# A hybrid decoder layer on one core: bias broadcasts moved into attention, half rows of x, and three small reorderings

## The chip, the core and the metric

The kernel runs on one core of a Trainium2 chip. A core has a matmul engine (TensorE, PE in the profile; its weight loads are PEld), three engines for elementwise work (VectorE, DVE; ScalarE, ACT; GpSimd, POOL), an engine that here only issues transfers (SyncE, SP), and 16 DMA engines that serve all transfer queues. Each engine works through its own queue in order, and semaphores make it wait for others. The metric is the device time of one execution in microseconds (us); lower is better.

## The reference

One layer (batch 1, 1024 tokens, width 1024, float32):

```python
h = rms_norm(x, attn_norm_w)
q, k, v, u, g = split(h @ w_in)                 # q, k: 8 heads x 2 halves x 64; v: 8 x 128
q, k = rms_norm(q), rms_norm(k)
p = softmax(q1 k1^T * scale + bias) - lam * softmax(q2 k2^T * scale + bias)   # causal; bias by T5 bucket of distance
a = rms_norm(p @ v, subln_w) * (1 - lam_init)
y_a = a @ w_proj_attn
c = silu(layer_norm(causal_depthwise_conv(u_a * sigmoid(u_b), conv_w, conv_b)))   # width 31
y_b = c @ w_proj_conv
x = x + (sigmoid(g_a) * y_a + sigmoid(g_b) * y_b) @ w_out
h = rms_norm(x, ffn_norm_w)
gt, up = split(h @ w_gate_up)                   # 2 x 2816 columns
x = x + (silu(gt) * up) @ w_down
```

## The kernel before

Every product is made of float32 operands split into a high and a low part (`split_hi` on ACT, L120; `split_lo` on DVE, L125, or on POOL in the first stage, L131); three matmuls (high x high, high x low, low x high) give one product. A set of weights is loaded (tile `wraw`, two buffers, or `room`), split into `whi` and `wlo`, and used. The large products, of u, of w_out and of the feed-forward part, are done with seven block products in place of eight, on sums and differences of 512 x 512 blocks; `T1` to `T4`, `S1` to `S4` are such sums. The program is unrolled. The order on each engine is set by a planner that simulates the program with its own estimates of durations; a block `with after(ins)` forces what is traced in it to stand behind `ins` on that engine's queue, and `last_of(engine)` is the instruction traced last on an engine.

The stages, with the times of the profiled execution:

- **First stage** (to about 310 us). RMSNorm and transposition of x to hT, then products of V and u, then the first of q, k. Between products, taps of the depthwise convolution (L595) fill DVE. A u item (`u_pair`) does seven products (L981); its weights are loaded by `prepare` (L945), summed by POOL (L962 to L965) and split. POOL also does the bias: it multiplies out the table of distances into b_d (8 heads x 1152), and `bias_skew(h)` (L777) broadcasts one head's row to the 128 rows of t_d[h], in DRAM, by a DMA from POOL's queue; there is one such issue per head, at every third step from n = 23 on. `add_tile` (L579) accumulates one convolution tile into cs_d, also from POOL's queue.
- **Attention** (to about 850 us). 64 steps (head h, row block i), n = 8h to 8h + 7 for head h, each with scores, exponentials, transposes of the probabilities (`turn`), and, for every two blocks, the product with V (`weigh`, tile pW). At a head's first step `load_bias(h)` reads t_d[h] with a skewed access (tile tb, L870). POOL only clears blocks of the transposed probabilities (L1318, L1319) and issues `add_tile`. Columns of g, of q and k of the later heads fill PE in between. SP loads v (vh, vl), weights, and the copies of q and k from partition to partition (qs, ks).
- **y_a and LayerNorm** (850 to about 920 us). `ya_out` (L1637) multiplies a finished product with its gate, which frees PE's bank; `ln_step` brings on steps of the LayerNorm, whose differences from the mean are L1570 and whose squares are L1571.
- **y_b, the gated merge** (to 1009 us), L1687 and L1688.
- **w_out** (1009 to 1095 us). Seven block products (L1843) in the order 11, 12, S1, S2, S4, S3, 22. `wload` fetches w_out's blocks (L1766; 16 transfers of 256 KB), `x_rows(l)` four blocks of 128 rows of x (L1778; 4 x 512 KB), `sload` the sums of the merge from DRAM (L1770); all are issued by SP. `wless` (L1774) makes a difference of blocks, four DVE instructions. After each product four sums x + wo (L1855) read PE's four banks; some are stored and squared for the next norm. `wo_banks` names the banks: the sum "b" lives in four banks of pool ps, "a" and then "c" in the four of pw. `norm2` scales and transposes rows for the next stage.
- **Feed-forward** (1095 us to the end), which the change does not touch. Its first GEMM (L168) takes banks of the tag pg, which the sum "b" of w_out has held.

## Time and profile before

| | |
|---|---|
| median of three runs | 1738.83 us (1737.25 to 1738.94) |
| the profiled execution | 1738.77 us, of which the program's span 1737.0 us |
| granted clock of TensorE, mean over the span | 0.999 |
| moved by DMA | 281.64 MB |

The span runs from the first to the last instruction of the program. A row of a list of waits reads: who waited, on which line and for which tile, for whom; the total, the number of waits and the longest. A row of a timeline reads: start, duration, engine, line, operation, tile written and tiles read, number of instructions merged, and, in brackets, the idle time before it and what ended it. A "q" behind an engine's name marks its issue queue.

### The profile page before, as it was taken

What the parts mean: (1) busy time and instruction counts of PE and PEld (TensorE: products, weight loads), DVE (VectorE), ACT (ScalarE), POOL (GpSimd) and SP (SyncE); (2) the same over time, 40 slices, a digit from 0 to 9 for tenths busy, and PEclk for the clock granted to TensorE, in tenths of its full rate; (3) what the DMA queues carried; (4) which work ended last, traced back from release to release, by engine and by line L of the source; (5) the groups of instructions that cost most, each with busy time, mean ns of one, the idle gap of its engine ahead of it and who ended that gap; (6) DMA issues with size and microseconds to landing.
All of it is one profiled execution on the core that took longest, in us unless ns stands there. A gap on an engine that the chain in (4) does not pass through costs nothing.

```text
span 1737.0 us, 25860 instructions
## 1 busy us (share of the span) xinstructions
PE 1717.4 (99%) x9245; PEld 1478.8 (85%) x9245; DVE 1275.2 (73%) x2128; ACT 863.3 (50%) x1958; POOL 218.6 (13%) x207
## 2 busy tenths in 40 slices
PE   9999999999999999999999999999999999999999
PEld 7997879998998998988788877888888888888887
DVE  7575879898988888878687768966676666565554
ACT  6333335667777777765566325633333333333332
POOL 4997761000000000000000000000000000000000
PEclk9999999999999999999999999999999999999999
DMA  6343546435435344443963683235445444598663
GB/s 202 118 133 121 178 137 166 117 92 146 117 109 148 108 116 128 105 134 132 337 234 122 200 302 104 74 105 180 152 158 174 154 152 150 175 361 280 216 218 132
DMA packets 260453, 281.64 MB, mean 162 GB/s; under 512 B 16418, under 2 KB 181858, under 8 KB 260324
## 3 DMA queue, kind: packets, MB, share of 16 engines
q1 hardware_dynamic: 254352, 269.55, 48.1%
q0 software_dynamic: 5680, 9.39, 2.5%
q8 instruction: 73, 1.20, 0.3%
q10 hardware_dynamic: 292, 1.05, 0.2%
q14 instruction: 56, 0.46, 0.1%
HBM read 181.84 MB, written 85.50 MB: 154 GB/s over the span
## 4 chain that ended last, share of the span: by engine, by line
PE 89%; DVE 4%; DMA 3%; ACT 2%; POOL 1%; issue 1%; SPq 0%; POOLq 0%
PE acc L981 28%; PE acc L489 12%; PE pg L168 12%; PE pg L169 11%; PE pg L170 11%; PE wo L1843 2%; PE sc L1290 2%; PE sc L1289 2%; PE pT L1328 2%; DVE acc L595 1%; PE pW L168 1%; PE pW L169 1%; PE pW L170 1%; PE pg L1107 1%; DMA wraw<-in_w_in_dram 1%
## 5 line engine op out<-in xcount | busy, mean ns | idle before, releaser
L595 DVE SCALAR_TENSOR_TENSOR acc<-u,cw,acc 128x1023 f32<-128x1023 f32 (+14 forms) x240 | 303.8, 1266 | 14.6 <-ACT acc L589 12.1
L168 PE MATMUL pg<-whi,hT_hi 128*128 128x256 f32 x704 | 199.7, 285 | 0.6 <-DVE v L125 0.6
L170 PE MATMUL pg<-whi,hT_lo 128*128 128x256 f32 x704 | 200.0, 285 | 0.0
L169 PE MATMUL pg<-wlo,hT_hi 128*128 128x256 f32 x704 | 199.3, 284 | 0.0
L125 DVE TENSOR_TENSOR wlo<-draw,whi 128x1024 fp32r<-128x1024 f32 x75 | 91.8, 1224 | 86.0 <-ACT whi L120 84.3
L120 ACT CAST whi<-draw 128x1024 fp32r<-128x1024 f32 x75 | 79.1, 1055 | 129.5 <-PE acc L489 117.6
L168 PEld LDWEIGHTS pg<-whi,hT_hi 128*128 128x128 f32 x704 | 134.0, 191 | 2.4 <-DVE v L125 0.8
L169 PEld LDWEIGHTS pg<-wlo,hT_hi 128*128 128x128 f32 x704 | 134.2, 191 | 1.7
L170 PEld LDWEIGHTS pg<-whi,hT_lo 128*128 128x128 f32 x704 | 134.2, 191 | 1.8
L120 ACT CAST whi<-wraw 128x1024 fp32r<-128x1024 f32 x90 | 94.6, 1051 | 69.3 <-PE pg L169 29.3
L489 PE MATMUL acc<-wlo,whi 128*128 128x512 f32 x308 | 119.8, 389 | 0.0
L489 PE MATMUL acc<-whi,wlo 128*128 128x512 f32 x308 | 119.8, 389 | 0.0
L1296 ACT ACTIVATE E<-E,mn 128x640 f32<-128x640 f32 (+7 forms) x128 | 99.8, 780 | 31.1 <-DVE mn L1291 29.4
L168 PE MATMUL pg<-hT_hi,whi 128*128 128x512 f32 x288 | 114.4, 397 | 0.1
L169 PE MATMUL pg<-hT_lo,whi 128*128 128x512 f32 x288 | 113.7, 395 | 0.0
L170 PE MATMUL pg<-hT_hi,wlo 128*128 128x512 f32 x288 | 113.6, 395 | 0.0
L120 ACT CAST whi<-s 128x1024 fp32r<-128x1024 f32 x54 | 56.8, 1053 | 108.7 <-PE acc L981 104.9
L125 DVE TENSOR_TENSOR wlo<-wraw,whi 128x1024 fp32r<-128x1024 f32 x75 | 92.7, 1239 | 14.0 <-ACT whi L120 13.8
L1291 DVE CUSTOM_DVE_ANT_0 E<-sc,tb 128x512 f32<-128x512 f32 (+3 forms) x128 | 74.5, 587 | 32.4 <-PE pT L1328 15.9
L981 PE MATMUL acc<-h_hi,whi 128*128 128x512 f32 x240 | 93.4, 389 | 0.0
L981 PE MATMUL acc<-h_lo,whi 128*128 128x512 f32 x240 | 93.4, 389 | 0.0
L981 PE MATMUL acc<-h_hi,wlo 128*128 128x512 f32 x240 | 90.1, 389 | 0.0
(370 smaller groups left out, 4594.8 us busy)
## 6 DMA issues: line engine op xcount, KB each, us to landing
wraw<-in_w_gate_up_dram SPq DMA_DIRECT2D x44, 512.0 KB, 4.7
wraw<-in_w_in_dram SPq DMA_DIRECT2D x40, 512.0 KB, 4.4
qs<-qs SPq DMA_DIRECT2D x96, 128.0 KB, 2.4
wd<-in_w_down_dram SPq DMA_DIRECT2D x44, 256.0 KB, 3.1
tdT<-wd SPq DMA_DIRECT2D x88, 128.0 KB, 4.8
draw<-sdS SPq DMA_DIRECT2D x44, 256.0 KB, 4.0
draw<-tdT SPq DMA_DIRECT2D x44, 256.0 KB, 3.9
wraw<-in_w_in_dram SPq DMA_DIRECT2D x32, 256.0 KB, 3.3
```

Source lines behind the costliest of these rows:

```text
L120: act.copy(dst, src)
L125: last_lo[0] = dve.tensor_tensor(dst, src, f32(hi), op=ALU.subtract).ins
L168: pe.matmul(o, lh, rh, start=start, stop=False)
L169: pe.matmul(o, lh, rl, start=False, stop=False)
L170: last_mm[0] = pe.matmul(o, ll, rh, start=False, stop=stop).ins
L489: m = pe.matmul(o[s_][i][:], l_[:, ts], r_[:, 512:], start=start and j + y_ == 0, stop=j == n - 1 and y_ == 2, skip_group_check=not start,)
L595: dve.scalar_tensor_tensor(a_, us[c][:, : S - n], cw[:, c, t : t + 1], a_, op0=ALU.mult, op1=ALU.add)
L981: last_mm[0] = pe.matmul(o[:], a_[x_][:, k, :], b_[y_][:, k, :], start=start and k + x_ + y_ == 0, stop=k == 3 and x_ == 1, skip_group_che ...
L1289: pe.matmul(o[:, :w], qh[:, qs], k, start=True, stop=False)
L1290: last_mm[0] = pe.matmul(o[:, :w], ql[:, qs], k, start=False, stop=True).ins
L1291: dve.tensor_tensor_reduce(e[:, ks], o[:, :w], tb[:, S - nk + c0 : S - nk + c0 + w], 1.0, mn[:, j : j + 1] if c0 else 3.0e38, ALU.add, ALU ...
L1296: act.activation(e[:, :nk], e[:, :nk], AF.Exp, bias=mn[:, j : j + 1], scale=-1.0, accum_out=l[:, j : j + 1])
```

## The change

1. `bias_skew` stays in the first stage for heads 0 and 1; those of heads 2 to 7 are issued in attention, at the third step of head h for head h + 2, behind the POOL instruction traced last.
2. The LayerNorm step behind the first two gated products must stand behind the first of these products on DVE (`gate_of[0, 0]`).
3. x is loaded in half rows (16 transfers of 256 KB in place of 8 of 512 KB): the first half of rows 0 to 511 ahead of w_out's fourth block (S4), the others spread among the sums.
4. The difference `wless("S3", "S4", "S3")` moves from the fourth product's second step to the fifth product's first.
5. The sum "b" takes its first two banks from the tag pg and its last two from pm, where it was the other way round.

```diff
-        if n >= 23 and n % 3 == 2 and (n - 23) // 3 < H:
+        if n >= 23 and n % 3 == 2 and (n - 23) // 3 < 2:
             with after(last_of(mybir.EngineType.Pool)):
                 bias_skew((n - 23) // 3)
...
         if n % NT == 0 and h:
             load_bias(h)
+        if n % NT == 2 and h + 2 < H:
+            with after(last_of(mybir.EngineType.Pool)):
+                bias_skew(h + 2)
...
-            dve.tensor_tensor(g[:], os2[sb][:], g[:], op=ALU.mult)
+            gate_of[c, sb] = dve.tensor_tensor(g[:], os2[sb][:], g[:], op=ALU.mult).ins
...
-    with after(first_gates):
+    with after(first_gates), after(gate_of[0, 0]):
         ln_step()
...
-    wo_banks = {"b": [(ps, "pm"), (ps, "pm"), (ps, "pg"), (ps, "pg")], "a": [(pw, "pw")] * 4, "c": [(pw, "pw")] * 4}
+    wo_banks = {"b": [(ps, "pg"), (ps, "pg"), (ps, "pm"), (ps, "pm")], "a": [(pw, "pw")] * 4, "c": [(pw, "pw")] * 4}
...
-    def x_rows(l):
+    def x_rows(l, c):
         for i in range(4 * l, 4 * l + 4):
-            nc.sync.dma_start(xa[i][:], xs[i * P : (i + 1) * P, :])
+            nc.sync.dma_start(xa[i][:, TOK[c]], xs[i * P : (i + 1) * P, TOK[c]])
...
                 wload("S1", (0, 0))
+                x_rows(0, 0)
                 wload("S4", (1, 1))
-                x_rows(0)
                 sload("S2")
+                x_rows(1, 1)
+                x_rows(0, 1)
                 sload("S4")
-                x_rows(1)
                 sload("S3")
+                x_rows(1, 0)
...
                     wless("22", "12", "S2")
-                    wless("S3", "S4", "S3")
                 for q in range(2):
                     early_weights("22", q, 2 * q)
+            if z == 4 and j == 0:
+                with after(last_lo[0]):
+                    wless("S3", "S4", "S3")
```

More of the change, by code (lines that the diff above doesn't have):

```diff
@@ L1631, in gated @@
         return g
+    gate_of = {}
     def ya_out(c, os2, gs=None):
```

## The prediction

> **What bounds the kernel now.** I read the page first, then the list of waits of the matmul engine, then the stretch around each wait, engine by engine.

> ```profile
> span 1737.0 us, 25860 instructions
> PE 1717.4 (99%) x9245; PEld 1478.8 (85%) x9245; DVE 1275.2 (73%) x2128; ACT 863.3 (50%) x1958; POOL 218.6 (13%) x207
> ```

> PE is busy 1717.4 of 1737.0 us. The change removes no matmul, so all that it can win lies in the 19.6 us in which PE stands still, and in matmuls that run at a lower clock. The profiled execution took 1738.77 us, 1.8 more than its span; the median of the runs is 1738.83, so the sum may start from either. The list of waits says where PE stands (total, times, longest):

> ```profile
> PE acc L981 <- POOL wlo L131: 4.0, 1, 4.0
> PE wo L1843 <- DVE xa L1855: 3.1, 2, 1.9
> PE wo L1843 <- DVE wlo L125: 1.6, 1, 1.6
> PE pg L168 <- DVE xa L1855: 0.7, 1, 0.7
> PE pg L168 <- DVE gt L1637: 0.5, 1, 0.5
> ```

> Together 9.9 us, and each of the five edits works at one of these rows. The first has a second part, seen in the stretches (length; busy time and count of PE, PEld, DVE, ACT, POOL; granted clock; DMA share; GB/s):

> ```profile
> 230.00:235.00 5.00, 5.00 (x16) 4.03 (x17) 2.66 (x3) 0.59 (x1) 2.18 (x1) 0.70 0.36 105
> 240.00:280.00 40.00, 40.00 (x275) 37.35 (x275) 32.92 (x33) 19.20 (x67) 14.05 (x12) 1.00 0.60 175
> 1030.00:1035.00 5.00, 2.55 (x11) 1.47 (x9) 5.00 (x9) 2.38 (x5) 0.00 (x0) 1.00 1.05 413
> ```

> After the 4.0 us stall the granted clock is 0.70 over 5 us: another 5 x 0.30 = 1.5 us. The 1.9 us stall near 1032 leaves it at 1.00.

> **Edit 1: six broadcasts of bias rows (t_d, issued by POOL) move from the first stage into attention.** POOL's queue now, at the place of the stall:

> ```profile
> 203.35 0.54 POOL L777 DMA_DIRECT2D t_d<-b_d  x1
> 205.15 0.54 POOL L777 DMA_DIRECT2D t_d<-b_d  x1
> 205.68 1.10 POOL L579 DMA_DIRECT2D cs_d<-c_d  x1
> 217.53 1.29 POOL L962 TENSOR_TENSOR s<-wraw 128x512 f32<-128x512 f32 x1 [8.33 <-DMA wraw<-in_w_in_dram]
> 227.50 2.35 POOL L131 TENSOR_TENSOR wlo<-wraw,whi 128x1024 fp32r<-128x1024 f32 x1
> ```

> POOL waited 8.3 us for a weight load, then worked through its queue, and the low part that PE wants came last, at 227.50 + 2.35 = 229.85, 4.0 us late. The DMA view of 203 to 218 us; its last row is the same pair of loads at 186 to 190 us, with no broadcast beside it:

> ```profile
> q0 software_dynamic: 816, 1.70, 42.3%
> q1 hardware_dynamic: 2371, 1.58, 36.5%
> t_d<-b_d POOLq DMA_DIRECT2D x2, 576.0 KB, 6.6
> wraw<-in_w_in_dram SPq DMA_DIRECT2D x2, 512.0 KB, 6.3
> ...
> wraw<-in_w_in_dram SPq DMA_DIRECT2D x2, 512.0 KB, 4.0
> ```

> Two broadcasts are 2 x 576 KB = 1.18 of the 1.70 MB on POOL's queue q0, which held the engines 0.423 x 15 = 6.3 us; by bytes 4.4 us of that is theirs (the packets of cs_d may be dearer per byte: at the 354 GB/s of a crowded stretch below 1.18 MB is 3.3 us). POOL also saves the 0.54 us issue at 203.35, ahead of work that frees the second load's buffer. So the load lands 3.8 to 4.9 us sooner; the stall needs 4.0. At either end 0.2 us of it or less stay, and the low clock goes with it: 4.0 + 1.5 = **5.5 us**. Is DVE late next? In 240 to 280 us it idles 40 - 32.9 = 7.1 us, more than 5.5, so it can follow.

> What the moved step brings to attention: six issues of 0.54 us on POOL, and per head 0.59 MB, 2.2 us of all engines at the share above. Each stands behind the memset of the step before (head 4 for example):

> ```profile
> 579.47 0.20 POOL L1318 MEMSET ph<- 128x128 f32 x1
> 600.97 0.21 POOL L1319 MEMSET pl<- 128x128 f32 x1 [21.30 <-PE pW L169]
> 583.37 0.54 SPq L1265 DMA_DIRECT2D vl<-v_lo  x1
> vl<-v_lo SPq DMA_DIRECT2D x1, 512.0 KB, 5.4
> 598.58 0.36 PE L168 MATMUL pW<-ph,vh 128*128 128x256 f32 x1
> ```

> POOL idles 21.3 us there, so the issue delays nobody. V's low half lands at 583.37 + 5.4 = 588.8 and is first needed at 598.58: 9.8 us of cover for 2.2 us. The broadcast itself is read two heads later. Cost 0; without that cover up to 2.2 us a head.

> **Edit 2: one product ahead of LayerNorm's differences.** DVE now:

> ```profile
> 851.88 0.68 DVE L1570 TENSOR_TENSOR lncsg<-cT_lo,mean 128x512 f32<-128x512 f32 x1
> 852.48 2.48 DVE L1637 TENSOR_TENSOR gt<-pg,gt 128x512 f32<-128x512 f32 x4
> 862.39 0.63 ACT L1571 ACTIVATE lnsq<-lncsg 128x512 f32<-128x512 f32 x1 [8.14 <-PE mean L1564]
> ```

> The differences (L1570) run first and the product that frees PE's bank comes behind them; reversed, the 0.5 us wait goes. The added wait holds back the differences and what DVE has behind them by the products, at most 2.5 us; their reader on ACT had idled 8.1 us. Gain **0.5**.

> **Edit 3: half rows of x ahead of w_out's fourth block; edit 4: the difference S3 later.** SP and DVE now:

> ```profile
> 1016.02 4.04 SPq L1766 DMA_DIRECT2D room<-in_w_out_dram  x6
> 1022.38 2.26 SPq L1778 DMA_DIRECT2D xa<-in_x_dram  x4
> 1027.80 2.49 DVE L1774 TENSOR_TENSOR room<-room,room 128x512 f32<-128x512 f32 x4
> 1030.20 3.08 DVE L1855 TENSOR_TENSOR xa<-wo,xa 128x512 f32<-128x512 f32 x5
> 1052.91 2.50 DVE L1774 TENSOR_TENSOR room<-room 128x512 f32<-128x512 f32 x4
> 1059.92 1.22 DVE L125 TENSOR_TENSOR wlo<-room,whi 128x1024 fp32r<-128x1024 f32 x1
> DMA packets 6042, 13.11 MB, mean 354 GB/s; under 512 B 671, under 2 KB 671, under 8 KB 6041
> ```

> The first product's four sums (x + wo) wait for x until 1030.2, when the second product ends as well, so eight sums of 3.08 / 5 = 0.62 us stand where four could. With x a transfer group earlier (four half rows, 1.05 MB, 3.0 us at 354 GB/s), the first four fit before 1027.8, and only the second product's four follow it. PE ran 11 matmuls in 2.55 us there (0.23 each), so it wants a bank, three matmuls, every 0.69 us: sums of 0.62 us keep up. The fourth block, last of the six issues that end at 1020.06, lands by 1025.5 if it takes the 5.4 us of the 512 KB load above; 3.0 us later that is 1028.5, so its difference (1027.80) starts 0.7 us late at most. I leave 0.4 us of the 3.1 standing for that: gain **2.7**. Behind the half rows on SP stand that block and the sums of m (soS); if SP must hold them for x's room, nothing is won here. The eight more issues cost SP 8 x 0.56 us, behind which only loads for much later products stand.

> Edit 4 takes 2.5 us (1052.91) out of DVE's queue ahead of the low part at 1059.92, which PE awaited 1.6 us. It comes back behind a later low part, for weights needed a product (48 matmuls of 0.23 us, 11 us) later. Gain **1.6**.

> **Edit 5: banks pg and pm swapped.**

> ```profile
> 1092.86 0.68 DVE L1855 TENSOR_TENSOR xa<-wo,xa 128x512 f32<-128x512 f32 x1
> 1094.05 1.88 DVE L1855 TENSOR_TENSOR xa<-wo,xa 128x512 f32<-128x512 f32 x3
> 1009.20 0.69 DVE L1687 TENSOR_TENSOR gt<-pg,gt 128x512 f32<-128x512 f32 x1 [2.64 <-PE pg L170]
> ```

> At the end the next GEMM wants a pg bank: now it is freed by the third sum (1094.05 + 2 x 0.62), after the swap by the first (1093.5): 0.7 gained. At the start w_out's first groups would take pg banks, one of which L1687 reads until 1009.89; at most its 0.69 us are lost there, nothing if that bank is not the first; I take the middle, 0.3. Net **0.4**.

> Sum: 5.5 + 0.5 + 2.7 + 1.6 + 0.4 = 10.7, so 1738.8 - 10.7 = 1728.1, **1728 us**.

> [...] The rows above move 13.11 MB, most of it in 256 KB pieces, at 354 GB/s. [...]

> **Rivals.** (a) *A part of it stays.* The planner sets each queue by its own estimates; if it puts the half rows where they wait for room, the 2.7 us are not won, and if the accumulation cs_d alone holds the load, some 2 us of the first stall stay, without the low clock: 1728.1 + 2.7 + 2.0 = 1732.8. For it: cs_d went in the same crowd. Against: the packets' share. [...] (b) *The half rows are slow*, at half the rate, 177 GB/s: the fourth block comes 3 us later still, the sums stay late and its difference costs 2 us: 1728.1 + 2.7 + 2.0 = 1732.8 as well. [...] (c) *Slower: the broadcasts meet attention's hand-over of q and k.* That one has no cover:

> ```profile
> 563.55 2.35 DMA ks<-klo
> 566.04 0.47 PE sc L1289
> ```

> k lands at 565.90 and PE starts 0.14 us later. A broadcast issued at the memset pair before this, not at 579.47, would delay it. Price per head: from 2.2 us to 8.33 / 2 = 4.2, POOL's wait at 217.53 shared among the two broadcasts in that crowd; at 3.2, six heads cost 19 us: 1747. It outweighs the gain from 10.7 / 6 = 1.8 us a head. Against: their place in POOL's order is 13 us behind it. (d) *The moves do nothing*, because the planner restores the old order or a new wait of equal size opens: 1738.

> **How the numbers follow.** Forecast 0.62 (with the bounds of its terms 1726 to 1730); (a) 0.16; (b) 0.02; (c) 0.11; (d) 0.09. The range reaches from 1725, for a little more than the sum (the runs shown differ by 1.7 us), over (a) and (b) to 1736; it leaves out (c) and most of (d). A measurement can tell about 0.2% (3.5 us): below 1735.3 is faster, 0.80; same 0.09; slower 0.11.

> **What would show it.** PE's list of waits loses all five rows or keeps under 1 us of each; the clock is 1.00 throughout 200 to 240; POOL's wait at L962 is under 5 us; the first sums run before 1028. It is wrong if the first row stays over 2 us, or if waits on ks, qs or V appear in attention.

## The result, and the profile after

| kernel | median | ratio to before, 95% interval | span of the profile |
|---|---|---|---|
| before | 1737.94 us (7 runs, 1735.74 to 1739.84) | | 1737.0 us |
| changed | 1733.59 us (7 runs, 1731.15 to 1734.47) | 0.9968 [0.9958, 0.9978] | 1730.3 us |

The change is faster by 0.32% by the ratio, 5.6 us, and the medians lie 4.4 us apart, where I had forecast 10.7. The profiled execution took 1732.11 us, 6.7 less than that of before. The head of the page:

```profile
span 1730.3 us, 25863 instructions
PE 1715.4 (99%) x9245; PEld 1477.7 (85%) x9245; DVE 1274.0 (74%) x2128; ACT 863.4 (50%) x1958; POOL 219.0 (13%) x207
```

PE's list of waits (total, times, longest):

```profile
PE wo L1852 <- DVE xa L1864: 3.3, 2, 2.7
PE pg L168 <- DVE gt L1692: 0.9, 1, 0.9
PE pg L168 <- ACT cT_hi L120: 0.8, 1, 0.8
PE sc L1290 <- DMA qs<-qs: 0.4, 1, 0.4
```

(Lines are 3 to 9 higher than in the kernel before: L1843 is now L1852, L1855 is L1864, L1774 is L1779.) Four of the five rows that I went after are gone: POOL's wlo (4.0), DVE's wlo (1.6), the end of w_out (0.7) and the first product (0.5). The fifth is as long as it was, 3.3 against 3.1. Two rows in the y_b stage are new, 0.9 and 0.8, near 940 us; before had none there.

The first stage went as drawn. POOL's timeline, at its wait for the weight load:

```profile
211.31 1.30 POOL L962 TENSOR_TENSOR s<-wraw 128x512 f32<-128x512 f32 x1 [3.06 <-DMA wraw<-in_w_in_dram]
```

The DMA queues in 203 to 218 us (packets, MB, share of the engines):

```profile
q1 hardware_dynamic: 2369, 1.57, 33.8%
q0 software_dynamic: 528, 0.52, 22.1%
```

The stretches where PE had stood (length; busy time and count of PE, PEld, DVE, ACT, POOL; granted clock; DMA share; GB/s):

```profile
225.00:230.00 5.00, 5.00 (x24) 4.14 (x23) 4.28 (x5) 1.22 (x2) 1.09 (x1) 1.00 0.35 103
230.00:235.00 5.00, 5.00 (x24) 4.14 (x23) 4.96 (x6) 2.73 (x3) 3.07 (x2) 1.00 0.00 0
```

L962 starts at 211.31 instead of 217.53, and PE is busy and at full clock throughout. In w_out nothing of the kind happened. SP's issue queue:

```profile
1017.82 2.28 SPq L1783 DMA_DIRECT2D xa<-in_x_dram  x4
```

DVE, from the landing of the first half row:

```profile
1022.95 0.69 DVE L1864 TENSOR_TENSOR xa<-wo,xa 128x512 f32<-128x512 f32 x1 [3.30 <-DMA xa<-in_x_dram]
1023.55 1.22 DVE L125 TENSOR_TENSOR wlo<-room,whi 128x1024 fp32r<-128x1024 f32 x1
1024.68 2.49 DVE L1779 TENSOR_TENSOR room<-room,room 128x512 f32<-128x512 f32 x4
1027.10 3.07 DVE L1864 TENSOR_TENSOR xa<-wo,xa 128x512 f32<-128x512 f32 x5
```

One sum runs early, and then DVE turns to a low part and to the four differences (L1779). The other sums stand behind these again, from 1027.10, when the second product is at its end. The half rows themselves went out at 1017.82, still behind all of w_out's blocks: the planner did not put them where the change has them in the program. Counted from w_out's first matmul, SP issues them 13.1 us on, against 13.4 for the whole rows of before.

### The profile page after: what moved, and what is told of

It is laid out like the page before. It is cut to its first block, busy times and chain, and to the rows that moved or that the text cites. A ratio compares the mean times of both kernels' runs of the same rounds, so it can differ in the third digit from the quotient of the medians.

```text
span 1730.3 us, 25863 instructions
## 1 busy us (share of the span) xinstructions
PE 1715.4 (99%) x9245; PEld 1477.7 (85%) x9245; DVE 1274.0 (74%) x2128; ACT 863.4 (50%) x1958; POOL 219.0 (13%) x207
## 3 DMA queue, kind: packets, MB, share of 16 engines
q10 hardware_dynamic: 292, 1.05, 0.2%
## 4 chain that ended last, share of the span: by engine, by line
PE 88%; DVE 5%; DMA 3%; ACT 2%; issue 1%; SPq 0%; ACTq 0%; DVEq 0%
PE acc L981 30%; PE acc L489 12%; PE pg L168 11%; PE pg L169 10%; PE pg L170 10%; PE wo L1852 3%; PE sc L1290 2%; PE sc L1289 2%; PE pT L1328 2%; DVE acc L595 1%; PE pW L169 1%; PE pW L168 1%; PE pW L170 1%; PE pg L1107 1%; PE pQ L816 1%
## 5 line engine op out<-in xcount | busy, mean ns | idle before, releaser
L168 PE MATMUL pg<-whi,hT_hi 128*128 128x256 f32 x704 | 199.7, 285 | 0.4 <-DVE v L125 0.4
L170 PE MATMUL pg<-whi,hT_lo 128*128 128x256 f32 x704 | 200.1, 285 | 0.0
L169 PE MATMUL pg<-wlo,hT_hi 128*128 128x256 f32 x704 | 199.4, 284 | 0.0
L125 DVE TENSOR_TENSOR wlo<-draw,whi 128x1024 fp32r<-128x1024 f32 x75 | 91.8, 1224 | 85.9 <-ACT whi L120 81.4
L120 ACT CAST whi<-draw 128x1024 fp32r<-128x1024 f32 x75 | 79.1, 1055 | 129.5 <-PE acc L489 119.3
L168 PEld LDWEIGHTS pg<-whi,hT_hi 128*128 128x128 f32 x704 | 134.0, 191 | 2.2 <-DVE v L125 0.6
L169 PEld LDWEIGHTS pg<-wlo,hT_hi 128*128 128x128 f32 x704 | 134.3, 191 | 1.8
L170 PEld LDWEIGHTS pg<-whi,hT_lo 128*128 128x128 f32 x704 | 134.2, 191 | 1.7
L168 PE MATMUL pg<-hT_hi,whi 128*128 128x512 f32 x288 | 114.4, 397 | 0.1
L169 PE MATMUL pg<-hT_lo,whi 128*128 128x512 f32 x288 | 113.7, 395 | 0.0
L170 PE MATMUL pg<-hT_hi,wlo 128*128 128x512 f32 x288 | 113.7, 395 | 0.0
L125 DVE TENSOR_TENSOR wlo<-wraw,whi 128x1024 fp32r<-128x1024 f32 x75 | 92.7, 1238 | 13.7 <-ACT whi L120 13.4
L981 PE MATMUL acc<-h_hi,whi 128*128 128x512 f32 x240 | 93.4, 389 | 0.0
L981 PE MATMUL acc<-h_lo,whi 128*128 128x512 f32 x240 | 93.4, 389 | 0.0
L981 PE MATMUL acc<-h_hi,wlo 128*128 128x512 f32 x240 | 90.1, 389 | 0.0
## 6 DMA issues: line engine op xcount, KB each, us to landing
wraw<-in_w_gate_up_dram SPq DMA_DIRECT2D x44, 512.0 KB, 4.8
wraw<-in_w_in_dram SPq DMA_DIRECT2D x40, 512.0 KB, 4.2
```

The costliest lines, as they stand in the source:

```text
L120: act.copy(dst, src)
L125: last_lo[0] = dve.tensor_tensor(dst, src, f32(hi), op=ALU.subtract).ins
L168: pe.matmul(o, lh, rh, start=start, stop=False)
L169: pe.matmul(o, lh, rl, start=False, stop=False)
L170: last_mm[0] = pe.matmul(o, ll, rh, start=False, stop=stop).ins
L981: last_mm[0] = pe.matmul(o[:], a_[x_][:, k, :], b_[y_][:, k, :], start=start and k + x_ + y_ == 0, stop=k == 3 and x_ == 1, skip_group_che ...
```

## The experiments

All ratios are to the kernel before.

**1. Edit 1 alone.** Before, with only the broadcasts moved.

> Only the six bias broadcasts are moved; everything else is as before. Theory (the broadcasts held the weight load): PE's 4.0 us on POOL's wlo goes, the granted clock is 1.00 from 200 to 240 us, and the other four rows of before (3.1, 1.6, 0.7, 0.5) stay; the span goes from 1737.0 to about 1731.5, the time to about 1733.3, ratio 0.9968. Rival (the accumulation cs_d held it): about 2 us of the first row stay, span about 1733.5. On the two new waits of the changed kernel near 940 us (0.84 on cT_hi, 0.93 on gt): if they come from edit 2's reorder they are absent here; if they come only from the earlier start that edit 1 brings, they are here too and the span is about 1733.

Measured: 1734.72 us, 0.9977 [0.9967, 0.9987], span 1733.7. The 4.0 us row is gone and neither new wait near 940 us is there: those do not come with edit 1. But the span fell by 3.3, not by 5.5. The lost part is at the old stall in w_out. Its row in PE's list of waits:

```profile
PE wo L1846 <- DVE xa L1858: 3.0, 2, 1.9
```

The stretches from there on:

```profile
1025.00:1028.40 3.40, 1.50 (x7) 1.05 (x6) 3.40 (x6) 2.38 (x5) 0.00 (x0) 1.00 1.04 405
1028.40:1031.80 3.40, 2.25 (x6) 1.58 (x6) 1.97 (x4) 1.33 (x4) 0.00 (x0) 0.50 1.04 419
1031.80:1035.20 3.40, 3.40 (x10) 2.63 (x9) 0.00 (x0) 0.00 (x0) 0.00 (x0) 0.50 1.03 405
```

The stall is no longer than before (3.0 against 3.1), yet 6.8 us at half the clock follow it, where before had 1.00. Experiment 9 takes this up.

**2. Only two of the six broadcasts moved**, those of heads 3 and 4:

```diff
-        if n >= 23 and n % 3 == 2 and (n - 23) // 3 < H:
+        if n >= 23 and n % 3 == 2 and (n - 23) // 3 < H and (n - 23) // 3 not in (3, 4):
...
+        if n % NT == 2 and h + 2 in (3, 4):
+            with after(last_of(mybir.EngineType.Pool)):
+                bias_skew(h + 2)
```

> The kernel of before with only the two broadcasts that were issued at 203.35 and 205.15 us (those of heads 3 and 4) moved into attention; the other six stay in the first stage. Theory (these two, beside the weight load, made the 4.0 us stall): the row PE acc on POOL wlo falls from 4.0 to under 0.5 us, as when all six are moved, and POOL's wait at L962 from 8.33 to about 3 us. Rival (it takes all six, since the earlier ones had put POOL behind): 2 us or more of the row stay. On the time: the same kernel without that row had a low clock once more near 1030 us, so the span may be 1731.5 (none) or 1733.7 (two low periods).

Measured: 1734.41 us, 0.9968 [0.9956, 0.998], span 1731.1. The row is gone entirely. POOL's wait:

```profile
210.29 1.28 POOL L962 TENSOR_TENSOR s<-wraw 128x512 f32<-128x512 f32 x1 [2.11 <-DMA wraw<-in_w_in_dram]
```

The two broadcasts beside the load made the stall; the other four cost nothing where they were. `cs_d`, issued beside the same load, still is, so the part of rival (a) that blamed it falls.

**3. The broadcasts at the hand-over of q and k.** The changed kernel with `n % NT == 6` in place of `n % NT == 2`.

> The changed kernel with each of the six broadcasts issued four steps later in its head, behind the zeroing near the hand-over to the next head (step 6 instead of step 2 of 8). Theory (my rival c: q and k have no cover at the hand-over, and a broadcast beside them delays them): rows PE sc on DMA ks or qs appear, 1.5 to 4 us for each head whose broadcast is issued within 3 us of the k loads, 3.2 in the middle; if all six, 19 us, span 1749; if half of them, 10 us, span 1740. Rival (the k loads are small and share well): under 0.5 us a head, span 1730 to 1733.

Measured: 1739.84 us, 1.0006 [0.9995, 1.0017], span 1738.2, against 1730.3 at the third step. PE's list of waits:

```profile
PE sc L1289 <- DMA ks<-klo: 4.5, 3, 3.0
PE pT L1328 <- ACT jk L1357: 1.1, 1, 1.1
PE sc L1289 <- DVE mn L1291: 0.6, 1, 0.6
```

The timeline ahead of the longest of them:

```profile
431.77 0.53 POOL L777 DMA_DIRECT2D t_d<-b_d  x1 [0.24 <-ACT ar L1342]
431.79 0.51 SPq L837 DMA_DIRECT2D ks<-klo  x1
```

And the stretches around it:

```profile
436.40:439.80 3.40, 0.90 (x5) 0.82 (x6) 1.01 (x2) 0.00 (x0) 0.00 (x0) 1.00 0.68 268
439.80:443.20 3.40, 3.40 (x16) 3.20 (x16) 3.18 (x8) 1.01 (x5) 0.00 (x0) 0.50 0.00 0
```

The mechanism of rival (c) exists and takes back all that the change won. Its price was too high: three heads of six waited for k, 2.95, 1.16 and 0.41 us (the last no longer than at the same place in some profiles with the broadcasts at the third step), and the worst of them, whose broadcast went out in the same moment as the k load, brought a low clock as well. By the ratios the six heads cost some 6.6 us more than at the third step (0.0038 x 1738), not 19.

**4. The changed kernel without edit 2.**

```diff
-    with after(first_gates), after(gate_of[0, 0]):
+    with after(first_gates):
         ln_step()
```

> The changed kernel without edit 2 (the LayerNorm step no longer waits for the first product). Theory (the planner's new order of the LayerNorm chain and of SP's queue, which came with edit 2, opened the waits near 940 us): the rows PE pg on ACT cT_hi (0.8) and PE pg on DVE gt L1692 (0.9) go, the 0.5 us wait at the first product comes back, span 1730.3 - 1.8 + 0.5 = 1729.0. Rival (edit 1 let PE run 6 us ahead of a LayerNorm chain that is bound by loads): the two waits stay at 1.8 together and the 0.5 comes back, span 1730.8.

Measured: 1731.24 us, 0.9953 [0.994, 0.9965], span 1729.0. Both waits near 940 us are gone and the 0.5 at the first product is back, as the first theory said. (The total of 1729.0 is partly chance: this profile holds 3.4 us of half clock at the w_out stall, a mean granted clock of 0.81 from 1025 to 1030 us and of 0.85 from 1030 to 1035, where the first profile of the changed kernel has 1.00.) How an edit at 850 us makes a wait at 940 shows on SP. The changed kernel:

```profile
920.36 0.38 SPq L302 DMA_DIRECT2D wraw<-in_w_proj_conv_dram  x1
920.84 0.53 SPq L1632 DMA_DIRECT2D gt<-g_d  x1
```

ACT there:

```profile
925.06 0.63 ACT L1633 ACTIVATE gt<-gt 128x512 f32<-128x512 f32 x1 [2.76 <-DMA gt<-g_d]
```

The same two transfers without edit 2:

```profile
918.52 0.32 SPq L1632 DMA_DIRECT2D gt<-g_d  x1
919.75 0.38 SPq L302 DMA_DIRECT2D wraw<-in_w_proj_conv_dram  x1
```

The new edge gave the planner another timetable, and in it a weight load stands ahead of a gate load. SP holds that load until DVE has freed its buffer (920.35), so the gate load goes out 2.3 us later. ACT, in order, waits for it 2.76 us, and the steps of LayerNorm behind it on ACT come late; PE catches up with their last outputs at 940 us. That is the row of 0.8. The row of 0.9 has another place. DVE in the changed kernel:

```profile
943.39 1.89 DVE L1692 TENSOR_TENSOR gt<-pg,gt 128x512 f32<-128x512 f32 x3 [1.43 <-PE pg L170]
```

DVE without edit 2:

```profile
939.40 0.69 DVE L1692 TENSOR_TENSOR gt<-pg,gt 128x512 f32<-128x512 f32 x1
942.46 1.29 DVE L1692 TENSOR_TENSOR gt<-pg,gt 128x512 f32<-128x512 f32 x2 [2.37 <-PE pg L170]
```

Two gated products changed places. In the changed kernel the one whose gate ACT has ready at 941.77 stands second, behind one that waits for PE until 943.37; it runs at 944.00, and its bank is the one that PE waits for. So this row comes from DVE's order and not from the late gate load: it is 0.9 in all six profiles with edit 2, while the other row goes from 0.8 down to 0.1.

**5. S2's differences later.** The changed kernel, with `wless("S2", "S4", "S1")` traced after the second product's sums and not in the middle of that product:

```diff
-            if z == 1 and j == 2:
-                with after(last_lo[0]):
-                    wless("S2", "S4", "S1")
...
+        if z == 1:
+            with after(last_add):
+                wless("S2", "S4", "S1")
```

> The changed kernel with one step moved: the four differences that make S2's weights stand on DVE behind the second product's sums instead of ahead of the first product's last three. x's loads stay where they are. Theory (DVE's order, not x, holds PE at 1030 us): the row PE wo on DVE xa falls from 3.3 us to at most 0.5, span 1730.3 - 2.9 = 1727.4, time about 1729.2. Rival (x's half rows still land too late): the sums wait for x, the row stays at 2 to 3.3 us, span about 1730. Third: the differences come too late for their own product, and a wait on a whi or wlo of room of up to 2 us appears near 1038 us.

Measured: 1729.14 us, 0.9946 [0.9932, 0.9959], span 1726.6. PE's row:

```profile
PE wo L1849 <- DVE xa L1861: 0.3, 1, 0.3
```

DVE:

```profile
1022.54 0.69 DVE L1861 TENSOR_TENSOR xa<-wo,xa 128x512 f32<-128x512 f32 x1 [3.32 <-DMA xa<-in_x_dram]
1023.15 1.22 DVE L125 TENSOR_TENSOR wlo<-room,whi 128x1024 fp32r<-128x1024 f32 x1
1024.28 4.27 DVE L1861 TENSOR_TENSOR xa<-wo,xa 128x512 f32<-128x512 f32 x7
1028.47 2.49 DVE L1779 TENSOR_TENSOR room<-room,room 128x512 f32<-128x512 f32 x4
```

With x arriving as in the changed kernel, seven sums in a row now run ahead of the differences, and 3.3 us of stall become 0.3. PE waits nowhere else in the 30 us that follow, so the differences do not come too late.

**6. w_out's fourth block behind the half rows**, as edit 3 is written:

```diff
                 x_rows(0, 0)
-                wload("S4", (1, 1))
+                with after(last_of(mybir.EngineType.SP)):
+                    wload("S4", (1, 1))
```

> The changed kernel with w_out's fourth block forced behind the first four half rows of x on SP, which is what edit 3 wrote and the planner did not do. Theory (DVE's order decides): the planner then puts the sums ahead of the differences, since the block that the differences read comes later, the row PE wo on DVE xa falls from 3.3 to under 1 us, although x itself lands no earlier than in the changed kernel (first half row 1022.9): span about 1727.5 to 1728. Rival (x's arrival decides): the row falls only if the first half row lands over 2 us sooner; landing at 1022.9, it stays near 3 us. Third (x must wait for its room): SP holds, block four and everything behind it comes later, and a wait of 1 to 3 us on the differences' weights appears near 1038 us.

Measured: 1730.34 us, 0.9948 [0.9936, 0.996], span 1727.2; the row falls to 0.7. SP's order is now the half rows, then the block, but the planner filled the place ahead of x with other loads, so the first half row comes no more than 0.8 us earlier (the first sum at 1022.14), and all of this profile runs about that much ahead there. What changed is DVE: five more sums run ahead of the differences, whose input now comes later. Same cure by another way.

**7. Without edit 2 and with S2's differences late** (4 and 5 together).

> The changed kernel without edit 2 and with the four differences of S2 behind the second product's sums. Theory (the two findings are independent): the waits near 940 us (0.9 on gt, up to 0.8 on cT_hi) go, 0.5 us at the first product comes back, the row PE wo on DVE xa stays at 0.3; span 1726.6 - 0.9 + 0.5 = 1726.2, time about 1728.5, within the noise of the better of the two. Rival (the planner's order near 940 us shifts again with the new plan): another wait of 0.5 to 1 us in 900 to 1000 us, span about 1727.5.

Measured: 1727.43 us, 0.9931 [0.9917, 0.9945], span 1726.2, as expected, and the time some 1 us less. Its five runs lie within 1.2 us (1727.22 to 1728.45).

**8. The same without edit 3**: x in whole rows, at the old place.

> The kernel of the run without edit 2 and with S2's differences late, now without edit 3 as well: x is loaded in whole rows (512 KB) at the old place. Theory (edit 3 brings x early enough, and is worth something once DVE's order uses it): whole rows land 1.2 us apart instead of 0.64, the last of the four at about 1027.4, so the second product's sums end later and PE waits 1.5 to 3 us on DVE xa near 1027 us instead of 0.4; span 1726.2 + 2 = 1728, plus 1.7 us if the clock falls after it. Rival (DVE's order is all, edit 3 is worth nothing): PE's wait stays at 0.4, span 1726.2.

Measured: 1727.22 us, 0.9934 [0.9918, 0.9951], span 1725.0. My theory falls, the rival holds. PE's row:

```profile
PE wo L1847 <- DVE xa L1859: 0.4, 1, 0.4
```

DVE, with all eight sums in one row:

```profile
1021.80 5.48 DVE L1859 TENSOR_TENSOR xa<-wo,xa 128x512 f32<-128x512 f32 x8
1027.20 2.49 DVE L1779 TENSOR_TENSOR room<-room,room 128x512 f32<-128x512 f32 x4
```

x comes hardly sooner than in before: its first row lands 18.7 us behind w_out's first matmul, there 19.1. With the differences first, PE waits 3.0 us with whole rows (experiment 1) and 3.3 with half rows; with the differences last, 0.4 with whole rows and 0.4 with half rows (experiment 7). Edit 3 is worth nothing either way. This version and the one above beat both kernels, that of before by some 11 us and the changed one by some 6, and can't be told apart.

**9. Why the clock fell: the same kernels profiled again.**

> The same kernel a third time, for the same question: the grid, counted in steps of 3.413 us from the clock's first rise near 10 us, tells which part of the stalls near 1027 us falls into one period; over 54% of one period idle, and the next is at half the clock.

> The changed kernel profiled once more. In its first profile the stall of 2.7 us near 1029 us lay across two periods of the grid, 48% of each, and the clock stayed up. Theory (grid): the stalls stay at 2.7 and 0.6 us, and in about 7 executions of 10 more than 54% of one period is idle and the next is at half the clock, span 1730.3 + 1.7 = 1732. Rival (a stall of 2.7 us never lowers it): span 1730.3 again, clock 1.00 after the stall.

Measured: edit 1 alone 1737.30 and 1735.24 us, each with a mean granted clock of 0.998, as in experiment 1; the changed kernel 1734.15 us, span 1732.4, now with two periods of half clock, 1028.9 to 1035.7 us. (The spans that I had put beside the number of periods were wrong: the 1733.7 of experiment 1 already held two.) The first profile of the changed kernel, in stretches of 3.40 us:

```profile
1025.30:1028.70 3.40, 1.73 (x8) 1.11 (x6) 3.40 (x7) 1.04 (x1) 0.00 (x0) 1.00 1.05 406
1028.70:1032.10 3.40, 1.77 (x7) 1.19 (x8) 3.40 (x6) 1.44 (x5) 0.00 (x0) 1.00 1.06 406
```

The second profile:

```profile
1025.50:1028.90 3.40, 1.38 (x7) 0.81 (x5) 3.40 (x7) 1.04 (x1) 0.00 (x0) 1.00 1.05 405
1028.90:1032.30 3.40, 2.27 (x5) 1.82 (x6) 3.40 (x6) 1.34 (x4) 0.00 (x0) 0.50 1.06 406
```

In the first, PE's idle time is split over two periods, 1.67 and 1.63 us (49 and 48%), and the clock stays; in the second, 2.02 us (59%) fall into one and the next is at half. The rival, that the length of the stall decides, is out: one stall of 2.7 us kept the clock here and one of 1.9 us kept it in before, while one of 1.9 us lost it in experiment 1 (0.50 over the next 6.8 us). The predicted 8 in 10 and 7 in 10 can't be told from three profiles.

**10. Edits 4 and 5 undone** in the changed kernel.

```diff
                     wless("22", "12", "S2")
+                    wless("S3", "S4", "S3")
...
-            if z == 4 and j == 0:
-                with after(last_lo[0]):
-                    wless("S3", "S4", "S3")
...
-    wo_banks = {"b": [(ps, "pg"), (ps, "pg"), (ps, "pm"), (ps, "pm")], "a": [(pw, "pw")] * 4, "c": [(pw, "pw")] * 4}
+    wo_banks = {"b": [(ps, "pm"), (ps, "pm"), (ps, "pg"), (ps, "pg")], "a": [(pw, "pw")] * 4, "c": [(pw, "pw")] * 4}
```

> The changed kernel with the difference S3 back at its old place (edit 4 undone) and the banks back (edit 5 undone). Theory (each edit owns its row): PE wo on DVE wlo comes back with 1.5 to 1.6 us near 1055 us, PE pg on DVE xa with 0.7 us near 1090 us, and the 0.1 us at the start of w_out goes; span 1730.3 + 2.2 = 1732.5. Rival (edit 3's half rows had moved DVE's queue so that these waits would be gone without edits 4 and 5): neither comes back, span 1730.

Measured: 1734.82 us, 0.9977 [0.9966, 0.9987], span 1732.7. Both rows came back at their size:

```profile
PE wo L1850 <- DVE wlo L125: 1.6, 1, 1.6
PE pg L168 <- DVE xa L1862: 0.7, 1, 0.7
```

The rival falls. Both edits were undone in one run; which of them owns which row follows from the places that they touch. That the span meets the expected 1732.5 is in part chance, for this profile has 2.5 us on DVE xa instead of 3.3; what made up for these 0.8 us the rows do not show.

## Why the prediction was right, and where it was wrong

The direction and the range (1725 to 1736) hold. The point, 1728, was 5.6 us too low, and two of its terms are why. Of the signs that I had named, these came: a clock of 1.00 from 200 to 240 us, POOL's wait at L962 under 5 us (3.06; in the other profiles without the two broadcasts 2.0 to 6.1), the first sums before 1028. One row stayed at 3.3 us, where I wanted all five under 1; and small waits on ks and qs appeared in attention, which I had called a sign of being wrong.

- **Edit 1, forecast 5.5: right.** The stall of 4.0 and the low clock behind it went; two broadcasts were the cause, as argued (experiment 2). I let the load land 3.8 to 4.9 us sooner. It let POOL go 6.2 us sooner in the changed kernel (211.31 against 217.53), 4.5 in experiment 1, and 3.7 to 7.6 over the 13 profiles without these two broadcasts, so the size held only roughly. In the changed kernel q0 held the engines 0.221 x 15 = 3.3 us instead of 6.3; that the load there gained more than these 3.0 us stays unexplained. The cost in attention, 0, holds to about 1 us: PE waited 0.2 us for ks and 0.4 for qs in the changed kernel, 0.1 together in before, and from nothing to 1.3 in the other profiles with broadcasts at the third step. These waits lie at 560 and 691 us and the nearest broadcasts at 573 and 635, so whether they come from them is open.
- **Edit 2, forecast a gain of 0.5: the row went, the price was missed.** The step "their reader on ACT had idled 8.1 us", hence no cost, looked at the instructions behind the new wait on DVE. The cost came from the planner, which set the queues of SP and DVE anew: 0.9 + 0.8 us near 940 (experiment 4). Over the profiles with edit 2 the first stays at 0.9, the second is between 0.1 and 0.8. By these rows it loses 0.5 to 1.2 us net. The ratios put it at 2.6 us, in experiment 4 as between 5 and 7, with intervals that overlap both times; what the rest would be, no run shows.
- **Edit 3, forecast 2.7: nothing won, the step that failed is its cause.** I wrote that the first four sums "wait for x until 1030.2". What ran on DVE until then stood in the fence above that sentence: the four differences, 1027.80 + 2.49 = 1030.29; and the stretch 1030 to 1035 shows DVE at 5.00 of 5.00. x's first row had landed at 1028.1, 2.1 us before the first sum. DVE's order was the bound, x was not (experiments 5, 6 and 8). The proviso "if SP must hold them for x's room" named a way to win nothing, though not this one.
- **Edit 4, 1.6: right. Edit 5, 0.4: right,** by the list 0.7 won at the end and 0.1 lost at the start, where I had taken 0.3. (Counted by the starts of matmuls the loss is 0.4: w_out's second product begins 11.28 us behind its first instead of 10.88. Matmuls of 0.39 us start every 0.23 us there (1009.00, 1009.23, 1009.46 in before), so an idle time in the list is shorter than what a stall costs.)
- **The clock: one reading was too wide.** From the stall of 4.0 us (0.70 over the 5 us behind it) and the one of 1.9 us (1.00) I took it that the shorter one does not lower the clock. In experiment 1 one of 1.9 us did, to 0.50 over 6.8 us.

So, by the list, 1728.1 + 2.7 + 0.2 for edit 3 + 1.8 for edit 2's new waits (0.93 and 0.84) - 0.2 for edit 5 makes 1732.6, against 1732.11 in the profile. The median is 1.5 above that profile, about one period of half clock (1.7 us); the second profile shows two such periods in w_out and the first none, which fits but was not measured for the other runs. Rival (a), 1732.8, hit the time by luck in part: the 2.7 were not won, though not because x waited for room, and cs_d cost nothing. On (b): with x in pieces of 256 KB the engines moved 402 to 406 GB/s from 1020 to 1040 us, in before, with pieces of 512 KB, 406 to 419, so the small pieces cost next to nothing here. The half rate, 177 GB/s, and the 2.0 us that (b) added for it were a supposition that no run shows.

## What to carry to other kernels

When a wait names an operand, look whether the engine that should produce it was idle or busy with something else. A producer that stands idle shortly before and is full during the wait, as DVE here (idle for 3.30 us up to 1022.95, busy 5.00 of 5.00 us from 1025), has an order problem; here the half rows did not help (0.4 us of stall with them and without, experiments 7 and 8). Where a planner orders every queue, an added edge has a cost in places that it does not touch, so compare the issue queues over the whole stage, not only the instructions beside the edge. Take a background transfer out from beside the one load that is on the path (POOL's wait for it fell from 8.33 to 3.06 us), and see what has no cover at its new place: four steps decided between 0.3% faster and no gain.

## What the runs showed of the hardware

In the trace of before the granted clock stands at 0.50 from 229.54 to 232.95 us, which is 3.413 us, and matmuls start every 0.43 us there and every 0.23 us behind it. Its record of the clock begins at 11.09 us, and 218.45 us, 64.0 times 3.413, lie from there to the fall. In the first profile of the changed kernel the record begins at 11.55 us, and the one fall, behind the last matmul, comes 1716.90 us later, 503.0 times. So in both the changes lie whole periods apart, from a start that was not the same.

In the profiles whose stretches were read period by period, the next period was at half the clock where PE had stood still for 100% of a period (before, 226.1 us), 74% (experiment 3, 436.4 us), 59% (second profile of the changed kernel, 1025.5 us) and 56% (experiment 1, 1025.0 us). It was at 1.00 where PE had stood still for 52% (before, 1031.7 us) and for 49 and 48% (first profile of the changed kernel, 1025.3 and 1028.7 us). A low period with PE idle for 34% (experiment 1) or 33% (second profile) was followed by another low one; those with 12% (before) and 0% (experiment 1 and second profile) were not (0.99, 1.00 and 0.99 behind them). The kernel before, with the stall of 4.0 us:

```profile
226.10:229.50 3.40, 0.00 (x0) 0.00 (x0) 3.37 (x4) 0.63 (x1) 3.40 (x3) 1.00 0.52 149
229.50:232.90 3.40, 3.00 (x7) 2.43 (x8) 3.16 (x3) 0.00 (x0) 2.68 (x2) 0.51 0.52 152
1031.70:1035.10 3.40, 1.62 (x6) 1.05 (x6) 3.40 (x6) 1.69 (x5) 0.00 (x0) 1.00 1.05 412
1035.10:1038.50 3.40, 2.83 (x12) 2.35 (x13) 1.11 (x2) 1.34 (x4) 0.00 (x0) 1.00 1.03 416
```

There the shorter stall put 1.78 us, 52%, into one period and got away with it. A stall of 1.9 us was followed by no low period there and by two in experiment 1; my estimate of what a low period costs is half of its 3.41 us, 1.7 us at most. Part of the spread of the times goes with this: the 23 runs of before beside experiments 2, 3, 7 and 10 lie over 8.6 us (1734.92 to 1743.51); the runs with a mean granted clock of 1.000 took 1735.7 to 1737.6, those with 0.996 or 0.997 took 1739.8 to 1743.5. The five of experiment 7, which has no stall near that length, lie over 1.2. It is not all of the spread: experiments 5 and 6, with stalls of 0.3 and 0.7 us there, lie over 3.0 and 2.7.
